# Sample attention: softmax sums from a column of ones, the key norms' root on GpSimd, latent products half a step later

## Chip, cores and metric

The kernel runs on one core of one Trainium2 chip. The metric is the device time of one execution in microseconds; the number of record is the median of several runs. The engines are named as in the profile: PE (TensorE matmul), DVE (VectorE), ACT (ScalarE), POOL (GpSimd), SP (SyncE, which issues the DMAs).

## What is computed

One inference step of a two-layer decoder for a prompt of 1024 tokens and for a sample group of 8 batches of 8 new tokens. The change lies almost wholly in one stage of layer 0, the attention of the sample group over its paged cache: per batch 16 pages of 128 keys, each key a latent row of 256 numbers and a rotary part of 32, and 8 heads with 8 queries each.

```python
def mla_core(qn, qr, k_nope, k_rope, c, mask, w_uv):
    s = (einsum('bqhd,bkhd->bhqk', qn, k_nope)
         + einsum('bqhr,bkr->bhqk', qr, k_rope)) * SOFTMAX_SCALE
    p = softmax(where(mask, s, -inf), axis=-1)
    lat = einsum('bhqk,bkc->bqhc', p, c)          # c: latent rows, 2048 old and 8 new
    return einsum('bqhc,chv->bqhv', lat, w_uv)
# k_nope = rms_norm(einsum('bkc,chd->bkhd', c, w_uk), g_k_nope): one root per key and head
```

## The kernel before

Products are made to float32's accuracy from pairs of float32r parts: x is split into a high part (a cast) and a low part (x minus the high part), and a product is the sum of three passes (`mm3`, L136).

In `sample_attention` a *page pair* is transposed on PE (`cpt`, L921), its high part `ch` is copied out by ACT (L924) and its low part `cl` made by DVE (L925). For each page `keys` runs 12 matmuls `pk` (L136): six of 256 columns and six of 320, ch and cl against the weights `wqh` and `wql`. ACT squares the keys (`psq`, L954), DVE sums the squares per head (`pss`, L956), and ACT copies the raw scores into `s`. After pages 7 and 15 `scale8` turns the 8 x 8 sums per key into 1 / rms (`rsqrt`), multiplies the scores of eight pages by it (`s<-s,prs`, L964) and adds the rotary scores (`s<-s,pr`, L966), which come from the products `pr` (L939).

`rsqrt` works on 128x64 numbers: `rsx` = ss / n + eps (L115), a first guess by a shift and a subtraction on the bits (`rst` L122, `rsr` L123), then three Newton steps of three DVE ops each (`rsu` L125, `rsu` L126, `rsr` or `prs` L127). Everything of it stands on DVE.

The softmax of batch b runs beside the keys of batch b + 1, dealt out by `slot` over 16 half-steps, q = 0 to 15 (half a page pair each). The maxima `smx` are taken over pages 0 to 7 (L973) and over the rest and the new keys (L980, L981, `soft1`); `soft2` transposes them on PE (`mxt`, L985) and makes a diagonal `sdg`; `soft3` spreads it by a product (`mxb`, L995), subtracts, exponentiates on ACT, splits the weights into `ph` (high and low part, 64 columns each) and sums them over the pages (`ssm`, L1004). `vsplit` splits a page's latent rows into `vh` (ACT, L1012) and `vl` (POOL, L1014; in the last batch mostly DVE) in four buffers in turn, at q = 3 to 11; `latent` adds the products of `ph` with `vh` and `vl` up in one PSUM bank (`lat`, L1027 and L1028), at q = 5 to 13, and the new keys' with `cs_h`, `cs_l`. `lat2` copies the bank to `ls`; `lat3` at q = 15 folds high and low part together (`lo`, two products with `i2`, the doubled identity, L1041), sums `ssm` over partitions by a product with ones (L1042), and DVE takes the reciprocal of 128x64 (`sri`, L1044) and multiplies by it into `latT` (L1046).

Each engine runs its list in order. The lists are set by a scheduler from the order in which the code is written and the dependences between tiles; a wait in a list holds up all that stands behind it on that engine.

Of the kernel before, what the change touches and what calls it, by code (L numbers as in the profile page):

```python
# [10 lines left out]
F32 = mybir.dt.float32  # L11
# [75 lines left out]
def wunit(g, ap, a, b, ring, lo=None):  # L87
    """One [128, a, b] block of a weight, split into two float32r parts that add up to it."""
# [10 lines left out]
def wcols(g, w, c0, c1, ring):  # L99
    """Columns c0:c1 of a [1024, n] weight as one unit of eight row blocks."""  # L100
    return wunit(g, w[:, c0:c1].rearrange("(k p) m -> p k m", p=P), KB, c1 - c0, ring)


def rsqrt(g, out, ss, inv_n, n, p=P):
    """out = (ss * inv_n + EPS) ** -0.5 on [p, n], to float32's accuracy."""
    v = g.nc.vector
    x = g.tiny.tile([P, 64], F32, name="rsx", tag="rsx")[:p, :n]
    t = g.tiny.tile([P, 64], I32, name="rst", tag="rst")[:p, :n]
# [13 lines left out]
    v.tensor_single_scalar(t, x.bitcast(I32), 1, ALU.logical_shift_right)  # L122
    v.tensor_scalar(r.bitcast(I32), t, -1.0, float(0x5F3759DF), ALU.mult, ALU.add)  # L123
# [6 lines left out]
def mm3(g, ps, pairs):  # L130
    """Accumulate float32 products of split operands: ((wh, wl), (xh, xl)) per row block."""
# [8 lines left out]
# ------------------------------------------------------------------ constants  # L140
# [19 lines left out]
def bcast_cols(g, ps, dg, r, out, n):  # L160
    """out[:, t * 128 + q] = r[q, t] on every partition: columns of per-token numbers as one row."""
# [7 lines left out]
# ------------------------------------------------------------------ feature-major norm  # L169
# The next product runs on x * gain; the row of 1 / rms, one number per token, multiplies its result.  # L170
# [48 lines left out]
# ------------------------------------------------------------------ MLP  # L219
# [46 lines left out]
class OutProj:  # L266
    """y += w.T @ X per chunk, then the operands and the scale of the next product."""
# [46 lines left out]
def in_even(g, I, O, S, st_left):  # L314
# [3 lines left out]
    with ExitStack() as st:  # L318
# [90 lines left out]
        def zproc(ci, tb0, nb, zs, sq):  # L409
# [34 lines left out]
            # latent and rotary key  # L444
# [12 lines left out]
            else:  # L457
                nc.sync.dma_start(O["ckv_s"][0].rearrange("b t d -> (b t) d"), cn[:p, 0])
                nc.sync.dma_start(O["kr_s"][0].rearrange("b t d -> (b t) d"), kr[:, 0])
                split(g, S.cs_h[:p], S.cs_l[:p], cn[:p, 0])  # L460
# [72 lines left out]
def pool_mixer(g, I, O, S, X, rs0, w, ps, ut, keep):  # L533
# [46 lines left out]
        # trailing window sums by doubling, the last group in two pieces  # L580
# [65 lines left out]
# ------------------------------------------------------------------ layer 0: keys and values  # L646
# [160 lines left out]
# ------------------------------------------------------------------ layer 0: sample attention  # L807
def sample_attention(g, I, S, ahead, fill_start, fill):
    nc = g.nc
    SQ = H * DT  # L810
    with ExitStack() as st:
# [17 lines left out]
        def load(b, pr):  # L829
            """Two pages of batch b."""  # L830
# [16 lines left out]
        # queries, feature-major  # L847
# [6 lines left out]
        # absorbed queries  # L854
# [13 lines left out]
        # moving operand [w_uk | absorbed queries], two copies in turn  # L868
# [6 lines left out]
        # block-diagonal rotary queries for four pages at once  # L875
# [52 lines left out]
        def ropes(b, q):  # L928
            """Rotary scores of pages 4 q .. 4 q + 3."""
# [12 lines left out]
        def keys(b, pg):  # L942
            """Keys of one page: sums of squares per head, and scores by absorbed queries."""
# [24 lines left out]
        mxs, ph_, sm_, pl_ = {}, {}, {}, {}  # L968
# [23 lines left out]
        def soft3(b, dg):  # L992
# [16 lines left out]
        def vsplit(b, pg):  # L1009
            ch = sa.tile([P, R], F32R, name="vh", tag="vh", bufs=4)  # L1010
            c_l = sa.tile([P, R], F32R, name="vl", tag="vl", bufs=4)
            nc.scalar.copy(ch, cps[b, pg])  # L1012
            e = nc.vector if b == DB - 1 and pg % 4 else nc.gpsimd
            e.tensor_tensor(c_l, cps.pop((b, pg)), ch.bitcast(F32), ALU.subtract)  # L1014
            vs[b, pg] = (ch, c_l)

        def latent(b, pg):
# [9 lines left out]
            nc.tensor.matmul(pl[:, :R], w, vh, start=(pg == 0), stop=False)  # L1027
# [4 lines left out]
        def lat2(b):  # L1032
            ls = sa.tile([P, R], F32, name="ls", tag="ls")
            nc.scalar.copy(ls, pl_.pop(b)[:, :R])
            lss[b] = ls

        def lat3(b):
            ls = lss.pop(b)
            po = msc("lo")
            for k in range(2):  # L1040
                nc.tensor.matmul(po[:, k * SQ:(k + 1) * SQ], ls[:, k * P:(k + 1) * P], i2, start=True, stop=True)  # L1041
            nc.tensor.matmul(po[:, 2 * SQ:3 * SQ], g.ones, sm_.pop(b), start=True, stop=True)  # L1042
            ri = sa.tile([P, SQ], F32, name="sri", tag="sri")
            nc.vector.reciprocal(ri, po[:, 2 * SQ:3 * SQ])  # L1044
            for k in range(2):
                nc.vector.tensor_tensor(latT[:, k, :, b * DT:(b + 1) * DT], po[:, k * SQ:(k + 1) * SQ].rearrange("p (h t) -> p h t", t=DT),  # L1046
                                        ri.rearrange("p (h t) -> p h t", t=DT), ALU.mult)

        def slot(b, q):
            """What the batch before does in half-step q (0..15) of the next one."""  # L1050
# [23 lines left out]
        for J in range(NJ + 8):  # L1074
# [31 lines left out]
            slot(b - 1, 2 * pr + 1)  # L1106
        fill()
# [11 lines left out]
# ------------------------------------------------------------------ layer 0: operands of the output projection  # L1119
# [44 lines left out]
def residual(g, y, xts, tb):  # L1164
    """The input's rows of one token block, feature-major."""
# [50 lines left out]
def rnn_prep(g, I):  # L1216
    """Vectors per channel and states, feature-major."""
# [49 lines left out]
def rnn(g, I, O, S, X, RS, gs, rp):  # L1267
    """gs[c][:, n] = gelu(gate) * h for every channel block n."""
# [11 lines left out]
    # the tiles that are free first come last in the pool, where the next phase's weights lie  # L1280
# [339 lines left out]
```

## Time and profile before

| | us |
|---|---|
| median of 3 runs | 2839.73 |
| lowest and highest run | 2837.73, 2841.03 |
| span of the profiled execution | 2838.5 |
| PE busy in it | 2713.7 (96%) |
| DVE, ACT, POOL busy | 1807.2, 898.8, 396.8 |

The sample attention takes the stretch from about 417 to 787 us of the span. Views by stretch (windows) give each engine's busy time in a piece of it; the groups by line say what an engine waited for just before an instruction; the timeline gives starts and durations of single instructions, and in brackets the idle time before one with what ended it. A matmul's duration includes its pipeline's depth, so what PE does per pass is read from the distance between starts, not from durations.

### The profile page before, as it was taken

Reading aid. Unit: us, or ns where it says so; the run is one execution under the profiler, and the core shown is the slowest. Engines: PE = TensorE matmul, PEld = TensorE weight load, DVE = VectorE, ACT = ScalarE, POOL = GpSimd, SP = SyncE. Lnnn points to the kernel's source line nnn. Section 1 sums busy time; section 2 is a strip of 40 time slices with the busy share of each in tenths; the row PEclk is TensorE's granted clock in tenths of the full one; section 3 lists DMA queues with packets and bytes.
Section 4 is the critical chain, followed back from the end, with each engine's and each line's share of the span. In section 5 each row is a group of like instructions: output and inputs, shape, how many; then the busy total and the mean of one; then the engine's idle time right before and its main releaser. Section 6 shows DMA issues by size and latency. Waiting matters only on the chain.

```text
span 2838.5 us, 43000 instructions
## 1 busy us (share of the span) xinstructions
PE 2713.7 (96%) x16801; PEld 2632.6 (93%) x16801; DVE 1807.2 (64%) x3501; ACT 898.8 (32%) x1878; POOL 396.8 (14%) x453
## 2 busy tenths in 40 slices
PE   7998999999999999999999998987999999999999
PEld 6887989888899999999999988887999999999998
DVE  7665657888755555555555579998365555555555
ACT  5334555666634111111111146655321111111111
POOL 4321001232212000000000044555200000000000
PEclk9999998999999999999999999998999999999999
DMA  5233102222251111111111121113111111111111
GB/s 161 62 108 108 38 16 76 62 61 59 70 136 42 45 45 46 42 49 39 49 40 48 36 90 35 35 31 109 47 47 50 39 48 39 49 38 51 38 38 64
DMA packets 200743, 162.07 MB, mean 57 GB/s; under 512 B 40331, under 2 KB 183148, under 8 KB 199763
## 3 DMA queue, kind: packets, MB, share of 16 engines
q1 hardware_dynamic: 200539, 159.31, 18.9%
q8 instruction: 133, 2.18, 0.3%
q14 instruction: 71, 0.58, 0.1%
HBM read 138.18 MB, written 21.21 MB: 56 GB/s over the span
## 4 chain that ended last, share of the span: by engine, by line
PE 62%; DVE 8%; ACT 1%; DMA 1%; POOL 1%; issue 1%; ACTq 0%; DVEq 0%; POOLq 0%
PE up L136 26%; PE dn L136 26%; PE op L136 6%; PE pgt L136 2%; DVE hs L1372 1%; DVE xl L182 1%; PE pg L136 1%; PE pu L136 1%; DVE v L1339 1%; DVE ta L1362 1%; DVE q L1392 0%; DVE y L250 0%; DVE vl L80 0%; ACT whA L79 0%; PE nbc L165 0%
## 5 line engine op out<-in xcount | busy, mean ns | idle before, releaser
L250 DVE TENSOR_TENSOR y<-y,dn 128x384 f32<-128x384 f32 (+1 forms) x768 | 404.9, 531 | 282.0 <-PE dn L136 279.7
L136 PE MATMUL dn<-hh,whB 128*128 128x384 f32 (+1 forms) x1536 | 505.8, 329 | 3.9 <-DVE y L250 3.8
L136 PE MATMUL up<-xh,wlA 128*128 128x384 f32 (+1 forms) x1536 | 501.6, 327 | 0.0
L136 PE MATMUL up<-xh,whA 128*128 128x384 f32 (+1 forms) x1536 | 501.1, 326 | 0.0
L136 PE MATMUL dn<-hh,wlB 128*128 128x384 f32 (+1 forms) x1536 | 501.0, 326 | 0.0
L136 PE MATMUL up<-xl,whA 128*128 128x384 f32 (+1 forms) x1536 | 501.0, 326 | 0.0
L136 PE MATMUL dn<-hl,whB 128*128 128x384 f32 (+1 forms) x1536 | 500.7, 326 | 0.0
L79 ACT CAST whB<-raw 128x1024 fp32r<-128x1024 f32 (+3 forms) x80 | 79.9, 1034 | 703.5 <-PE dn L136 663.4
L136 PEld LDWEIGHTS dn<-hh,whB 128*128 128x128 f32 x1536 | 288.3, 188 | 11.8 <-DVE y L250 11.6
L136 PEld LDWEIGHTS up<-xh,wlA 128*128 128x128 f32 x1536 | 288.3, 188 | 0.4
L136 PEld LDWEIGHTS up<-xh,whA 128*128 128x128 f32 x1536 | 288.3, 188 | 0.3
L136 PEld LDWEIGHTS dn<-hl,whB 128*128 128x128 f32 x1536 | 288.4, 188 | 0.1
L136 PEld LDWEIGHTS up<-xl,whA 128*128 128x128 f32 x1536 | 288.3, 188 | 0.2
L136 PEld LDWEIGHTS dn<-hh,wlB 128*128 128x128 f32 x1536 | 288.3, 188 | 0.0
L235 DVE SCALAR_TENSOR_TENSOR rl<-up,rs 128x384 f32<-128x384 f32 (+1 forms) x192 | 102.8, 535 | 260.3 <-PE up L136 260.3
L236 ACT ACTIVATE hh<-rl 128x384 fp32r<-128x384 f32 (+1 forms) x192 | 97.1, 506 | 447.7 <-DVE rl L235 447.7
L80 POOL TENSOR_TENSOR wlA<-raw,whA 128x1024 fp32r<-128x1024 f32 (+2 forms) x24 | 58.4, 2435 | 769.2 <-ACT whA L79 766.7
L136 PE MATMUL pk<-wqh,cl 128*128 128x256 f32 (+1 forms) x512 | 153.3, 305 | 12.7 <-DVE cl L925 12.6
L136 PE MATMUL pk<-wqh,ch 128*128 128x320 f32 (+1 forms) x512 | 160.1, 315 | 0.7 <-ACT ch L924 0.7
L79 ACT CAST whA<-raw 128x1024 fp32r<-128x1024 f32 (+2 forms) x94 | 98.0, 1042 | 184.8 <-PE up L136 143.2
L237 DVE TENSOR_TENSOR rl<-rl 128x384 f32<-128x384 f32 (+1 forms) x192 | 106.0, 552 | 77.5 <-ACT hh L236 77.5
L136 PE MATMUL pk<-wql,ch 128*128 128x256 f32 (+1 forms) x512 | 151.9, 298 | 1.2 <-DVE wql L80 1.2
(558 smaller groups left out, 5378.5 us busy)
## 6 DMA issues: line engine op xcount, KB each, us to landing
raw<-in_w_up_dram SPq DMA_DIRECT2D x64, 512.0 KB
raw<-in_w_down_dram SPq DMA_DIRECT2D x64, 512.0 KB
cp<-in_cache_ckv_dram SPq DMA_DIRECT2D x128, 128.0 KB
raw<-in_w_in_rnn_dram SPq DMA_DIRECT2D x16, 512.0 KB
xt<-in_x_prompt_dram SPq DMA_DIRECT2D x8, 512.0 KB
raw<-in_w_out_even_dram SPq DMA_DIRECT2D x8, 512.0 KB
raw<-in_x_prompt_dram SPq DMA_DIRECT2D x8, 512.0 KB
raw<-in_w_out_rnn_dram SPq DMA_DIRECT2D x8, 512.0 KB
```

The lines of the kernel that those rows point to most:

```text
L79: g.nc.scalar.copy(h, src)
L80: (lo or g.nc.vector).tensor_tensor(l, src, h.bitcast(F32), ALU.subtract)
L136: g.nc.tensor.matmul(ps, a, b, start=(i == 0), stop=(i == n - 1))
L182: nc.vector.scalar_tensor_tensor(xl[:, m], yv, gcol[:, m:m + 1], xh[:, m].bitcast(F32), ALU.mult, ALU.subtract)
L235: nc.vector.scalar_tensor_tensor(r[:, :n], ps[:, :n], 0.0, RS[c][:, :n], ALU.max, ALU.mult)
L236: nc.scalar.activation(hh[:, a:b], r[:, :n], AF.Square)
L237: nc.vector.tensor_tensor(r[:, :n], r[:, :n], r[:, :n], ALU.mult)
L250: nc.vector.tensor_tensor(y[c][:, m], y[c][:, m], ps[:, :n], ALU.add)
L1339: V.scalar_tensor_tensor(v, ul[:, a + k:b + k], vec[:, k, n:n + 1], v, ALU.mult, ALU.add)
L1362: V.scalar_tensor_tensor(ta[:, a:b], a0[:, a:b], 1.0, ta[:, a:b], ALU.add, ALU.mult)
L1372: V.tensor_tensor_scan(hs[:, a:b], a0[:, a:b], ig[:, a:b], hs[:, a - 1:a] if a else 0.0, ALU.mult, ALU.add)
```

## The change

- `rsqrt`: the shift and the subtraction on the bits become one op (`rsr` from `rsx`, a multiplication by -0.5 and an addition), for all its users. With an engine given, as `scale8` does, the three Newton steps are made of four ops each on GpSimd (three products and one op that scales and adds), 12 in all, since there the op with two operations and two tensors is not used.
- Softmax sums: the tiles of the latent rows' high parts get two columns of ones (`VT`, four fixed pairs of tiles in turn, filled once; `cs_h` likewise), so the `lat` products of `vh` have 258 columns, and the last two hold the sums of the weights. The reduction `ssm` and its product with ones go. `lat3` folds the sums by a small product (`lf`, with the new constant `fold`), takes a reciprocal of 128x1 and scales the doubled identity by it (`i2s`). The folding products `lo` then use `i2s`, in a new step `lat4` at q = 2 of the batch after, with one copy into `latT` in place of two products on DVE.
- Times: `latent` runs at q = 6 to 14 (before 5 to 13) and is written ahead of `vsplit`, now at q = 4 to 11 (before 3 to 11); `lat2` at 14 (before 13).

```diff
+    v.tensor_scalar(r.bitcast(I32), x.bitcast(I32), -0.5, float(0x5F3759DF), ALU.mult, ALU.add)
+    if eng is not None:
+        for it in range(3):
+            eng.tensor_tensor(u, r, r, ALU.mult)
+            eng.tensor_tensor(u, u, x, ALU.mult)
+            eng.tensor_scalar(u, u, -0.5, 1.5, ALU.mult, ALU.add)
+            eng.tensor_tensor(out if it == 2 else r, u, r, ALU.mult)
+        return
...
-            rsqrt(g, r, ss, 1.0 / QN, 64)
+            rsqrt(g, r, ss, 1.0 / QN, 64, eng=nc.gpsimd)
...
-            sm = sa.tile([P, SQ], F32, name="ssm", tag="ssm")
-            nc.vector.tensor_reduce(sm, s.rearrange("p a q -> p q a"), AX.X, ALU.add)
...
+            ch, c_l = vs[b, pg] = VT[pg % 4]
+            nc.scalar.copy(ch[:, :R], cps[b, pg])
...
-            nc.tensor.matmul(pl[:, :R], w, vh, start=(pg == 0), stop=False)
+            nc.tensor.matmul(pl[:, :R + 2], w, vh, start=(pg == 0), stop=False)
...
+            nc.tensor.matmul(pf[:, :2], fold.rearrange("p a q -> p (a q)"), lss[b][:, R:], start=True, stop=True)
+            ri = g.tiny.tile([P, 1], F32, name="sri", tag="sri", bufs=2)
+            nc.vector.reciprocal(ri, pf[:, 0:1])
+            i2s = sa.tile([P, NS], F32, name="i2s", tag="i2s")
+            nc.vector.tensor_scalar_mul(i2s, i2, ri)
...
+                nc.tensor.matmul(po[:, k * SQ:(k + 1) * SQ], ls[:, k * P:(k + 1) * P], i2s, start=True, stop=True)
+            nc.vector.tensor_copy(latT[:, :, :, b * DT:(b + 1) * DT],
+                                  po[:, :2 * SQ].rearrange("p (k h t) -> p k h t", k=2, t=DT))
...
+            if q == 2 and b >= 1:
+                lat4(b - 1)
...
-            if 5 <= q <= 13:
-                for pg in range(2 * (q - 5), 2 * (q - 5) + 2):
+            if 6 <= q <= 14:
+                for pg in range(2 * (q - 6), 2 * (q - 6) + 2):
```

The scheduler then sets other lists. DVE in the middle of a batch, before (Newton chain from `rsx` on; `cl` is the low part of pair 29's latents, which PE waits for):

```order
L925 TENSOR_TENSOR cl<-cpt,ch 128x512
L956 TENSOR_REDUCE pss<-psq 128x8
L115 TENSOR_SCALAR rsx<-pss 128x64
L122 TENSOR_SCALAR rst<-rsx 128x64
L123 TENSOR_SCALAR rsr<-rst 128x64
L125 TENSOR_TENSOR rsu<-rsr 128x64
L126 SCALAR_TENSOR_TENSOR rsu<-rsu,rsx 128x64
L127 SCALAR_TENSOR_TENSOR rsr<-rsu,rsr 128x64
L956 TENSOR_REDUCE pss<-psq 128x8
L125 TENSOR_TENSOR rsu<-rsr 128x64
L925 TENSOR_TENSOR cl<-cpt,ch 128x512
```

The same place in the list of the changed kernel:

```order
L938 TENSOR_TENSOR cl<-cpt,ch 128x512
L969 TENSOR_REDUCE pss<-psq 128x8
L114 TENSOR_SCALAR rsx<-pss 128x64
L122 TENSOR_SCALAR rsr<-rsx 128x64
L969 TENSOR_REDUCE pss<-psq 128x8
L977 TENSOR_TENSOR s<-s,prs 128x512
L938 TENSOR_TENSOR cl<-cpt,ch 128x512
L979 TENSOR_TENSOR s<-s,pr 128x512
```

The steps between `rsr` and the product have left DVE's list, and the product that needs their result now stands ahead of the second `cl`.

POOL's list there, in the changed kernel (the last Newton step, then the low parts of pages 8 and on; before, the list held `vl` alone there):

```order
L125 TENSOR_TENSOR rsu<-rsr 128x64
L126 TENSOR_TENSOR rsu<-rsu,rsx 128x64
L127 TENSOR_SCALAR rsu<-rsu 128x64
L128 TENSOR_TENSOR prs<-rsu,rsr 128x64
L1024 TENSOR_TENSOR vl_4920<-cp,vh_4919 128x256
L1024 TENSOR_TENSOR vl_4922<-cp,vh_4921 128x256
```

So the low parts behind the chain run only when it is done; those of pages 4 to 7 stand ahead of it.

PE at the boundary between two batches, before: the transposed maxima `mxt` stand among the `cpt` transposes of the fourth page pair of the next batch, behind 62 `pk` passes of it:

```order
L136 MATMUL pk<-wqh_4916,cl 128x320
L921 MATMUL cpt<-ident,cp 128x128 x3
L985 MATMUL mxt<-ident,smx 64x128
L921 MATMUL cpt<-ident,cp 128x128
L136 MATMUL pk<-wqh_4916,cl 128x256
```

And in the changed kernel, in the middle of the fourth page, behind 45 `pk` passes:

```order
L142 MATMUL pk<-wqh_4891,ch 128x320
L142 MATMUL pk<-wql_4892,ch 128x320
L142 MATMUL pk<-wqh_4891,cl 128x320
L998 MATMUL mxt<-ident,smx 64x128
L142 MATMUL pk<-wqh_4891,ch 128x320
L142 MATMUL pk<-wql_4892,ch 128x320
```

`mxt` moved ahead by 17 `pk` passes and three transposes.

## Rows read from the trace of the kernel before

**Rows 1.** The page's head and its first part: busy time, share of the span and instructions of each engine.

```profile
span 2838.5 us, 43000 instructions
...
PE 2713.7 (96%) x16801; PEld 2632.6 (93%) x16801; DVE 1807.2 (64%) x3501; ACT 898.8 (32%) x1878; POOL 396.8 (14%) x453
```

**Rows 2.** Timeline of PE at the transposed maxima of one batch (start, duration, engine, line, operation, operands).

```profile
568.18 0.30 PE L985 MATMUL mxt<-ident,smx 128*64 128x128 f32 x1
```

**Rows 3.** Windows of some 41 us in the stage: stretch and its length, then busy time and count of PE, PE's weight loads, DVE, ACT and POOL, the granted clock of PE, the DMA share and GB/s.

```profile
566.00:607.00 41.00, 38.47 (x277) 35.72 (x276) 33.91 (x67) 26.20 (x83) 12.21 (x18) 1.00 0.23 59
```

**Rows 4.** Groups of PE's instructions by line in one batch, 568.18 to 609.70: busy time, mean ns | idle time just before them and what ended it.

```profile
L136 PE MATMUL pk<-wqh,cl 128*128 128x256 f32 (+1 forms) x64 | 19.0, 302 | 1.5 <-DVE cl L925 1.5
...
L1028 PE MATMUL lat<-vl,ph 128*128 128x256 f32 x16 | 4.5, 302 | 0.8 <-POOL vl L1014 0.7
...
L985 PE MATMUL mxt<-ident,smx 128*64 128x128 f32 x2 | 0.6, 298 | 0.3
```

**Rows 5.** Timeline of PE in that batch, around its middle and at its end (in brackets idle time before, and what ended it).

```profile
577.28 0.28 PE L1027 MATMUL lat<-vh,ph 128*128 128x256 f32 x1
578.25 0.39 PE L1028 MATMUL lat<-vl,ph 128*128 128x256 f32 x1 [0.70 <-POOL vl L1014]
...
582.71 0.28 PE L1028 MATMUL lat<-vl,ph 128*128 128x256 f32 x1
582.83 0.28 PE L1027 MATMUL lat<-vh,ph 128*128 128x256 f32 x1
...
583.30 0.28 PE L136 MATMUL pk<-wql,ch 128*128 128x256 f32 x1
585.13 0.39 PE L136 MATMUL pk<-wqh,cl 128*128 128x256 f32 x1 [1.55 <-DVE cl L925]
...
598.64 0.59 PE L939 MATMUL pr<-qbd,kpT 128*128 128x256 f32 x2
599.08 0.55 PE L1041 MATMUL lo<-i,ls 128*128 128x64 f32 x4
...
599.66 0.36 PE L136 MATMUL pk<-wqh,ch 128*128 128x256 f32 x1
...
601.34 0.60 PE L921 MATMUL cpt<-ident,cp 128*128 128x128 f32 x4
601.70 0.36 PE L136 MATMUL pk<-wqh,ch 128*128 128x256 f32 x1
...
606.57 0.31 PE L136 MATMUL pk<-wqh,ch 128*128 128x320 f32 x1
...
609.70 0.30 PE L985 MATMUL mxt<-ident,smx 128*64 128x128 f32 x1
```

**Rows 6.** Timeline of DVE in the middle of the batch.

```profile
578.14 0.67 DVE L956 TENSOR_REDUCE pss<-psq 128x8 f32<-128x512 f32 x1
578.84 0.43 DVE L115 TENSOR_SCALAR rsx<-pss 128x64 f32<-128x64 f32 x1
579.31 2.93 DVE L122 TENSOR_SCALAR rst<-rsx 128x64 int32<-128x64 int32 x1
...
584.39 0.68 DVE L925 TENSOR_TENSOR cl<-cpt,ch 128x512 fp32r<-128x512 f32 x1
...
586.49 0.22 DVE L127 SCALAR_TENSOR_TENSOR prs<-rsu,rsr 128x64 f32<-128x64 f32 x1
```

**Rows 7.** Timeline of POOL beside it.

```profile
579.36 2.82 POOL L1014 TENSOR_TENSOR vl<-cp,vh 128x256 fp32r<-128x256 f32 x4
```

**Rows 8.** Timeline of DVE behind the last batch: the second op of the first Newton guess, the first and the last of nine Newton ops that follow each other undisturbed, the last maximum, the sums of the weights.

```profile
765.03 0.18 DVE L122 TENSOR_SCALAR rst<-rsx 128x64 int32<-128x64 int32 x1
...
765.48 0.23 DVE L125 TENSOR_TENSOR rsu<-rsr 128x64 f32<-128x64 f32 x1
...
767.55 0.23 DVE L127 SCALAR_TENSOR_TENSOR prs<-rsu,rsr 128x64 f32<-128x64 f32 x1
...
777.02 2.11 DVE L1004 TENSOR_REDUCE ssm<-s 128x64 f32<-128x1088 f32 x1
```

**Rows 9.** One line of layer 1 on POOL, a product of two tensors of 128x64: least, median and greatest duration in ns, first and last start.

```profile
L1398 POOL TENSOR_TENSOR y<-q,hs x8: 305/617/636, 1758.0 to 1960.2; 128x64 f32<-128x64 f32 x8
```

**Rows 10.** Group of POOL's copies of the new keys' scores (busy us, mean ns | idle before).

```profile
L978 POOL COPY s<-snew 64x64 f32<-64x64 f32 x8 | 1.9, 238 | 2.8 <-DVE snew L904 2.7
```

**Rows 11.** Timeline of POOL: two ops on the same tile, one behind the other.

```profile
418.62 0.28 POOL L899 TENSOR_SCALAR_AFFINE_SELECT msk<-msk 64x64 f32<-64x64 f32 x1
418.97 0.28 POOL L900 TENSOR_SCALAR_AFFINE_SELECT msk<-msk 64x64 f32<-64x64 f32 x1
```

**Rows 12.** Timeline of DVE at the boundary between two batches.

```profile
599.26 0.69 DVE L956 TENSOR_REDUCE pss<-psq 128x8 f32<-128x512 f32 x1 [0.35 <-ACT psq L954]
...
605.36 0.69 DVE L964 TENSOR_TENSOR s<-s,prs 128x512 f32<-128x512 f32 x1
...
607.76 1.16 DVE L980 TENSOR_REDUCE smx<-s 128x64 f32<-128x576 f32 x1
...
609.43 0.21 DVE L981 TENSOR_TENSOR smx<-smx 128x64 f32<-128x64 f32 x1
```

**Rows 13.** Timeline of PE behind the last batch, up to its maxima.

```profile
771.23 0.66 PE L1174 MATMUL xtp<-ident,raw 128*128 128x128 f32 x2 [1.60 <-DMA raw<-in_x_prompt_dram]
771.68 0.42 PE L985 MATMUL mxt<-ident,smx 128*64 128x128 f32 x1
```

More of the change, by code (lines that the diff above doesn't have):

```diff
@@ L101, in wcols, with rsqrt @@
     return wunit(g, w[:, c0:c1].rearrange("(k p) m -> p k m", p=P), KB, c1 - c0, ring)
-def rsqrt(g, out, ss, inv_n, n, p=P):
+def rsqrt(g, out, ss, inv_n, n, p=P, eng=None):
     v = g.nc.vector
     x = g.tiny.tile([P, 64], F32, name="rsx", tag="rsx")[:p, :n]
-    t = g.tiny.tile([P, 64], I32, name="rst", tag="rst")[:p, :n]
     u = g.tiny.tile([P, 64], F32, name="rsu", tag="rsu")[:p, :n]
@@ L121, in rsqrt @@
         return
-    v.tensor_single_scalar(t, x.bitcast(I32), 1, ALU.logical_shift_right)
-    v.tensor_scalar(r.bitcast(I32), t, -1.0, float(0x5F3759DF), ALU.mult, ALU.add)
+    v.tensor_scalar(r.bitcast(I32), x.bitcast(I32), -0.5, float(0x5F3759DF), ALU.mult, ALU.add)
[6 more added lines that the diff above has]
+        return
     for it in range(3):
@@ L459, in zproc @@
                 nc.sync.dma_start(O["kr_s"][0].rearrange("b t d -> (b t) d"), kr[:, 0])
-                split(g, S.cs_h[:p], S.cs_l[:p], cn[:p, 0])
+                split(g, S.cs_h[:p, :R], S.cs_l[:p], cn[:p, 0])
+                nc.gpsimd.memset(S.cs_h[:p, R:].bitcast(F32), 1.0)
             later(g, lambda: latents(tb0, nb, p, cn))
@@ L887, in sample_attention @@
         nc.vector.tensor_copy(i2[NS:], g.ident[NS:, NS:])
+        fold = sa.tile([P, 2, NS], F32, name="fold", bufs=1)
+        nc.gpsimd.tensor_copy(fold, i2[:, None, :].to_broadcast([P, 2, NS]))
+        VT = [(sa.tile([P, R + 2], F32R, name=f"vh{i}", bufs=1), sa.tile([P, R], F32R, name=f"vl{i}", bufs=1)) for i in range(4)]
+        for vh, _ in VT:
+            nc.gpsimd.memset(vh[:, R:].bitcast(F32), 1.0)
         latT = sa.tile([P, 2, H, NS], F32, name="latT", bufs=1)
@@ L966, in scale8 @@
             nc.vector.tensor_tensor(sf, sf, pr8[b].rearrange("p a q -> p (a q)"), ALU.add)
-        mxs, ph_, sm_, pl_ = {}, {}, {}, {}
+        mxs, ph_, pl_ = {}, {}, {}
         HF = ((0, 8), (8, NPG + 1))
@@ L1002, in soft3 @@
                 nc.vector.tensor_tensor(ph[:, x:y, 1], sv, ph[:, x:y, 0].bitcast(F32), ALU.subtract)
-            sm = sa.tile([P, SQ], F32, name="ssm", tag="ssm")
-            nc.vector.tensor_reduce(sm, s.rearrange("p a q -> p q a"), AX.X, ALU.add)
-            ph_[b], sm_[b] = ph, sm
+            ph_[b] = ph
         vs = {}
         def vsplit(b, pg):
-            ch = sa.tile([P, R], F32R, name="vh", tag="vh", bufs=4)
-            c_l = sa.tile([P, R], F32R, name="vl", tag="vl", bufs=4)
-            nc.scalar.copy(ch, cps[b, pg])
+            ch, c_l = vs[b, pg] = VT[pg % 4]
+            nc.scalar.copy(ch[:, :R], cps[b, pg])
             e = nc.vector if b == DB - 1 and pg % 4 else nc.gpsimd
-            e.tensor_tensor(c_l, cps.pop((b, pg)), ch.bitcast(F32), ALU.subtract)
-            vs[b, pg] = (ch, c_l)
+            e.tensor_tensor(c_l, cps.pop((b, pg)), ch[:, :R].bitcast(F32), ALU.subtract)
         def latent(b, pg):
@@ L1032, in lat2, with lat4 @@
         def lat2(b):
-            ls = sa.tile([P, R], F32, name="ls", tag="ls")
-            nc.scalar.copy(ls, pl_.pop(b)[:, :R])
+            ls = sa.tile([P, R + 2], F32, name="ls", tag="ls")
+            nc.scalar.copy(ls, pl_.pop(b)[:, :R + 2])
             lss[b] = ls
         def lat3(b):
-            ls = lss.pop(b)
+            pf = msc("lf")
+            nc.tensor.matmul(pf[:, :2], fold.rearrange("p a q -> p (a q)"), lss[b][:, R:], start=True, stop=True)
[3 more added lines that the diff above has]
+            nc.vector.tensor_scalar_mul(i2s, i2, ri)
+            lss[b] = lss[b], i2s
+        def lat4(b):
+            ls, i2s = lss.pop(b)
             po = msc("lo")
             for k in range(2):
[L1041 to L1047, printed above, removed]
+                nc.tensor.matmul(po[:, k * SQ:(k + 1) * SQ], ls[:, k * P:(k + 1) * P], i2s, start=True, stop=True)
+            nc.vector.tensor_copy(latT[:, :, :, b * DT:(b + 1) * DT],
+                                  po[:, :2 * SQ].rearrange("p (k h t) -> p k h t", k=2, t=DT))
         def slot(b, q):
+            if q == 2 and b >= 1:
+                lat4(b - 1)
             if b < 0:
@@ L1056, in slot @@
                 soft3(b, st_.pop(b))
-            if 3 <= q <= 11:
-                for pg in range(2 * (q - 3), min(2 * (q - 3) + 2, NPG)):
-                    vsplit(b, pg)
-            if 5 <= q <= 13:
-                for pg in range(2 * (q - 5), 2 * (q - 5) + 2):
+            if 6 <= q <= 14:
+                for pg in range(2 * (q - 6), 2 * (q - 6) + 2):
                     if pg <= NPG:
                         latent(b, pg)
-            if q == 13:
+            if 4 <= q <= 11:
+                for pg in range(2 * (q - 4), 2 * (q - 4) + 2):
+                    vsplit(b, pg)
+            if q == 14:
                 lat2(b)
@@ L1106, in sample_attention @@
             slot(b - 1, 2 * pr + 1)
+        lat4(DB - 1)
         fill()
@@ L1446, in step @@
         S.kr = l0p.tile([P, NTB, QR], F32, name="kr")
-        S.cs_h = l0p.tile([P, R], F32R, name="cs_h")
+        S.cs_h = l0p.tile([P, R + 2], F32R, name="cs_h")
         S.cs_l = l0p.tile([P, R], F32R, name="cs_l")
```

## Prediction

> **What bounds the kernel now.** I read the page's head first: TensorE (PE) is busy 96% of the span [rows 1], so only stages in which it waits can give or take time. The change touches one stage, the sample attention: 8 batches of 16 pages, about 41.5 us a batch (the transpose `mxt` of one batch stands at 568.18, that of the next at 609.70) [rows 2, 5]. There PE is busy 38.5 of 41 us, VectorE (DVE) 33.9 and GpSimd (POOL) 12.2, at a granted clock of 1.00, the 2.4 GHz level [rows 3]. PE runs its list in order, so a batch is the sum of its passes and of its waits. The groups of one batch name the waits: 1.5 us for DVE's `cl`, 0.7 to 0.8 for POOL's `vl`, 0.3 at the two `mxt` [rows 4]. Matmul starts show a little more: `lat` passes that otherwise follow 0.12 us apart stand 0.97 apart at 578.25, and the `pk` pass on `cl` comes 1.83 after its neighbour at 585.13, 1.7 too late [rows 5]. With smaller hitches of the `lat` passes just before, I put the `vl` waits at 1.7 us, the `cl` wait at 1.7, and at the boundary between batches some 0.4. All that the change can win is therefore about 4 us in each of 7 or 8 batches, near 30 us.
>
> Both larger waits lie in the middle of a batch. DVE gets `rsx` at 578.84; the next Newton step `rst`, 0.2 us of work, takes 2.93 while POOL runs four `vl` (579.36, 2.82 us), and `prs` ends at 586.7. `cl` was put inside this chain and is done only at 585.07 [rows 6, 7].
>
> **The Newton chain on GpSimd** is the term that decides. Two chains a batch (16 in all) lose 10 ops on DVE and get 12 on POOL: 9 with two inputs, 3 with one, each waiting for the one before. On DVE nine steps run from 765.48 to 767.78, 2.30 us [rows 8]. No POOL op of this kind on 128x64 stands in this stage. Nearest is `y<-q,hs` on 128x64: least 305 ns, median 617 [rows 9]; for one input the 64x64 copy with 238 ns [rows 10]. Two dependent POOL ops start 0.35 apart when one takes 0.28, so 0.07 goes to each hand-over [rows 11]. I take the least of 305, since DVE mostly idles while it waits for this chain: 9 x 0.375 + 3 x 0.31 = 4.3 us. Bounds: 12 x 0.31 = 3.7 if all cost as the copy, 12 x 0.69 = 8.2 if all cost the median. The chain is thus some 2 us longer than DVE's undisturbed one.
>
> **The boundary.** Let t count from the `pr` pass behind page 15 (598.64). Before, `pss` is done at 1.3, the product `s<-s,prs` starts at 6.7, since `pss` and `cl` are mixed into the chain, and the last maximum is done at 11.0, 0.06 before `mxt` [rows 5, 12]. After: `pss` 1.3; with the small reciprocal, its scaling, `rsx` and `rsr`, POOL can start at 2.25; chain to 6.6; product, sum, a `pss`, the 1.16 us maximum, a `pss`, the last maximum: 6.65 + 0.7 + 0.7 + 0.6 + 1.1 + 0.6 + 0.2 = 10.5. So `mxt` is ready half a microsecond earlier than before. But in the new order PE reaches it earlier by far: between page 15 and `mxt` stand 45 `pk` passes, where there were 62. Three pages of 1.68, two sets of `cpt` transposes of 0.36 and nine passes more reached 606.57 in the old trace, t = 7.9, and the two `lo` passes fewer bring it to 7.5 [rows 5]. PE waits 3.0 us there, 2.6 more than now. `cl` of the next pair stands behind the last maximum, but only some 0.7 us behind, so it is just in time. The first `lat` may then wait 0.3 for `ph`.
>
> **The middle.** t counts from the end of page 7's products. `pss` to 1.3; POOL still has `vl` of pages 6 and 7 ahead of the chain, whose fixed tiles come free only behind PE's `lat` passes of pages 2 and 3, so it starts at 2.3 to 2.6 and ends at 6.6 to 6.95. DVE's list has the product `s<-s,prs` ahead of `cl`, so `cl` is done at 8.3. PE gets there at 5.7: `pr` 0.5, eleven `lat` passes of 0.12, two pages of 1.68, four `cpt` 0.36 and two passes [rows 5]. It waits 2.55 instead of 1.7. The longer chain stays in this place, in front of the same matmul. The `vl` of pages 8 and on are queued behind the chain on POOL; their first reader stands a page behind the late `cl` (9.8 against 7.7), so that costs nothing unless the chain grows by 2 us.
>
> **What is taken away.** Latents half a step later and tiles with fixed turns: the `vl` wait of 1.7 us should go, since `vl` of pages 4 to 7 now run ahead of the chain and PE asks later. The 2.11 us reduction `ssm` leaves DVE [rows 8], as do the two reciprocals' worth of work at the boundary; on DVE only the part before a `cl` counts, and the waits above have it already. PE saves two passes a batch, 0.2 us. Constants and four fills of ones: once, on an idle POOL, nothing; `lat` passes of 258 columns for 256: 17 x 1 ns, nothing; one op fewer in nine other roots: under 0.2 us each, beside matmuls.
>
> **The tail.** Behind the last batch the POOL chain is on the path, 1.4 to 2 us longer, but PE waits 1.60 for a DMA just ahead of `mxt` [rows 13], and without `ssm` the last `vl` and `lat` come 2 us earlier; the extra pass through `lf`, reciprocal and `lo` gives 1 back. I take +0.5, from -1 to +1.5.
>
> **The sum**, against the profiled execution: span 2838.5 [rows 1], 1.2 below the median 2839.73. Boundary 7 x 2.6 = +18.2; `ph` 7 x 0.3 = +2.1; middle 8 x 0.85 = +6.8; `vl` 7 x 1.7 = -11.9; PE passes -1.4; tail +0.5: **+14.3 us**, 2852.8 of span, 2854 as a median. Every microsecond of the chain counts in both places of nearly every batch, 15 us. It comes out even at a chain of 3.35 us, 0.28 an op with its hand-over.
>
> **Rivals.**
> *The POOL chain is short, or PE's new place fits it (faster, 2828).* At 2.6 us, DVE's pace, the sum is 14.3 - 1.7 x 15 = -11. For it: the rough spans of POOL, and a DVE that is relieved of 4 us a batch, so that `cl` and `pss` come earlier everywhere. Against it: no two-input row under 305 ns. The floor, with all waits gone, is near 2810.
> *It cancels (within 0.2%, 2840).* A chain of 3.7 us, the lower bound, gives 14.3 - 9 = +5, just inside; likewise if the 2.93 us hold of `rst` was costlier than I count.
> *POOL and DVE hinder each other (slower, 2872 and more).* `y<-q,hs` takes 617 ns in its median, and `rst` shows the reverse case. If the first third of each chain, beside `pss` and `cl`, runs at the median, the chain grows by 4 x 0.31 = 1.2 us: +18, 2872. From a chain of 6.3 us on, `vl` is late as well, and the waits it was to lose return: 2890.
> *A step's rule.* At 64 columns POOL takes 305 ns where DVE takes 225 [rows 8, 9], 1.36 times as long. If it were twice as long, 9 x (0.45 + 0.07) + 3 x 0.31 = 5.6 us of chain give 14.3 + 1.3 x 15 = +34, 2874. The Trainium skill ("GPSIMD Engine Reference", 4.1 Engine selection) says just that, GpSimd about two times slower than VectorE for elementwise work with two inputs, and that such work belongs on VectorE; the least of the row above speaks for a milder factor at this width.
> *It does nothing,* since the stage is not on the path: nothing runs beside PE's list that could hide its waits, so this has no chance of its own and lies in the even case.
>
> **How the numbers follow.** Forecast case (2844 to 2864) 0.43; engines that hinder each other 0.12, the factor of two 0.10; even 0.14; faster 0.21. Slower than 2845.4, that is by over 0.2%, about what a measurement of this kernel can tell from no change: 0.65. Same 0.14, faster 0.21. The range leaves out the extremes of the dear cases and the deep end of the faster one: 2827 to 2875.
>
> **What would show it.** Right: PE groups with a wait of about 3 us at `mxt` and 2.5 at `cl`, both a batch, released by DVE; `vl` gone from PE's releasers; a chain of 12 POOL ops over 4.3 us; the last maximum at t = 10.5; a period near 43.5 us. Wrong: POOL steps under 0.28 us, or above 0.45; `mxt` with no wait (then the new order was well placed, and the kernel is faster by the `vl` waits alone); new waits for `vl` at pages 8 to 11, or for `lo`.

## The result, and the profile after

The changed kernel takes **2872.24 us** (median of 4 runs, 2871.3 to 2875.18), the kernel before 2838.73 beside it (4 runs, 2837.24 to 2841.03): ratio **1.0121, 95% interval 1.0106 to 1.0135**, 33.5 us slower. Slower was forecast, and 2872 lies in the range, near its end; the size was more than double the forecast of 14.3.

| | before | after |
|---|---|---|
| span of the profiled execution | 2838.5 us | 2869.5 us |
| mean granted clock of PE over the span | 0.976 | 0.969 |
| from `mxt` to `mxt`, the batch of [rows 2] | 41.52 us | 47.61 us |
| idle of PE before `mxt`, 8 of them | 0.9 us | 22.1 us |
| idle of PE before `pk` on `cl`, whole span | 12.7 us | 22.4 us |
| idle of PE before `lat` on `vl`, whole span | 5.3 us | 0.7 us |

The page's head and its first part, after, beside [rows 1]:

```profile
span 2869.5 us, 43004 instructions
...
PE 2716.9 (95%) x16801; PEld 2642.4 (92%) x16801; DVE 1750.7 (61%) x3324; ACT 897.7 (31%) x1878; POOL 452.7 (16%) x651
```

PE's busy time rose by 3.2 us although the number of its instructions is the same (two `lf` products of a batch stand where two products with ones stood): something made passes longer. The groups of PE over the whole span, before and then after (idle time of PE just before the group, and what ended it):

```profile
L136 PE MATMUL pk<-wqh,cl 128*128 128x256 f32 (+1 forms) x512 | 153.3, 305 | 12.7 <-DVE cl L925 12.6
L1028 PE MATMUL lat<-vl,ph 128*128 128x256 f32 x128 | 35.9, 302 | 5.3 <-POOL vl L1014 3.7 <-DVE vl L1014 0.9
L985 PE MATMUL mxt<-ident,smx 128*64 128x128 f32 x8 | 2.5, 311 | 0.9 <-DVE smx L981 0.3
```

```profile
L142 PE MATMUL pk<-wqh,cl 128*128 128x256 f32 (+1 forms) x512 | 160.2, 316 | 22.4 <-DVE cl L938 22.4
L1037 PE MATMUL lat<-vl,ph 128*128 128x256 f32 x128 | 37.0, 309 | 0.7 <-POOL vl L1024 0.5
L998 PE MATMUL mxt<-ident,smx 128*64 128x128 f32 x8 | 2.9, 360 | 22.1 <-DVE smx L994 22.1
```

So the `vl` waits went, and two larger ones stand in their place, both ended by DVE. The timeline of PE around them, to be held against [rows 5] (start, duration, operands; in brackets idle time before):

```profile
591.95 0.58 PE L142 MATMUL pk<-wqh,cl 128*128 128x256 f32 x1 [2.87 <-DVE cl L938]
592.33 0.41 PE L142 MATMUL pk<-wqh,ch 128*128 128x256 f32 x1
592.54 0.41 PE L142 MATMUL pk<-wql,ch 128*128 128x256 f32 x1
...
608.53 0.59 PE L952 MATMUL pr<-qbd,kpT 128*128 128x256 f32 x2
...
618.91 0.42 PE L998 MATMUL mxt<-ident,smx 128*64 128x128 f32 x1 [2.75 <-DVE smx L994]
618.99 0.61 PE L142 MATMUL pk<-wqh,ch 128*128 128x320 f32 x1
619.40 0.47 PE L142 MATMUL pk<-wql,ch 128*128 128x320 f32 x1
```

Read not only the brackets but the passes behind them: the 128x256 passes follow 0.21 us apart, where the kernel before has 0.12. The windows of these places name the reason (busy times, then the granted clock, ahead of the DMA share and GB/s):

```profile
588.80:592.00 3.20, 0.34 (x4) 0.13 (x2) 1.90 (x3) 0.76 (x3) 2.95 (x7) 0.90 0.04 14
592.00:594.50 2.50, 2.50 (x10) 2.50 (x11) 2.04 (x3) 0.38 (x1) 1.26 (x2) 0.50 0.37 103
...
619.00:621.50 2.50, 2.50 (x12) 2.50 (x13) 1.59 (x4) 0.75 (x3) 0.00 (x0) 0.50 0.00 0
```

0.50 is the 1.2 GHz level: PE was idle for most of 3 us, and the passes behind ran at half rate. The kernel before waits 1.55 us at the first place [rows 5] and its passes behind run at 1.00.

The chain itself, on POOL (its first step, and its last op with the four `vl` queued behind it), and DVE beside it, to be held against [rows 6, 12]:

```profile
585.61 0.29 POOL L125 TENSOR_TENSOR rsu<-rsr 128x64 f32<-128x64 f32 x1
585.99 0.32 POOL L126 TENSOR_TENSOR rsu<-rsu,rsx 128x64 f32<-128x64 f32 x1
586.39 0.25 POOL L127 TENSOR_SCALAR rsu<-rsu 128x64 f32<-128x64 f32 x1
586.72 0.33 POOL L128 TENSOR_TENSOR rsr<-rsu,rsr 128x64 f32<-128x64 f32 x1
...
589.75 0.32 POOL L128 TENSOR_TENSOR prs<-rsu,rsr 128x64 f32<-128x64 f32 x1
590.02 3.24 POOL L1024 TENSOR_TENSOR vl<-cp,vh 128x256 fp32r<-128x256 f32 x4
```

```profile
590.10 1.20 DVE L977 TENSOR_TENSOR s<-s,prs 128x512 f32<-128x512 f32 x1 [3.21 <-POOL prs L128]
591.22 0.68 DVE L938 TENSOR_TENSOR cl<-cpt,ch 128x512 fp32r<-128x512 f32 x1
...
615.10 0.69 DVE L977 TENSOR_TENSOR s<-s,prs 128x512 f32<-128x512 f32 x1 [2.37 <-POOL prs L128]
...
618.64 0.21 DVE L994 TENSOR_TENSOR smx<-smx 128x64 f32<-128x64 f32 x1
```

From 585.61 to 590.07 the chain takes 4.46 us; 4.3 was forecast. Meanwhile DVE stands 3.21 us before the product `s<-s,prs`, and `cl`, which needs nothing from the chain, stands behind it in DVE's list.

### The profile page after: what moved, and what is told of

Read it like the earlier page. It is cut to its first block, busy times and chain, and to the rows that moved or that the text cites. A ratio compares the mean times of both kernels' runs of the same rounds, so it can differ in the third digit from the quotient of the medians.

```text
span 2869.5 us, 43004 instructions
## 1 busy us (share of the span) xinstructions
PE 2716.9 (95%) x16801; PEld 2642.4 (92%) x16801; DVE 1750.7 (61%) x3324; ACT 897.7 (31%) x1878; POOL 452.7 (16%) x651
## 4 chain that ended last, share of the span: by engine, by line
PE 61%; DVE 8%; ACT 1%; issue 0%; POOL 0%; DMA 0%; ACTq 0%; DVEq 0%; SPq 0%; POOLq 0%
PE up L142 26%; PE dn L142 26%; PE op L142 6%; PE pgt L142 1%; DVE hs L1390 1%; DVE xl L188 1%; DVE v L1357 1%; PE pu L142 1%; PE pg L142 1%; DVE ta L1380 1%; DVE q L1410 0%; DVE vl L80 0%; DVE y L256 0%; PE otp L1569 0%; DVE t L1372 0%
## 5 line engine op out<-in xcount | busy, mean ns | idle before, releaser
L142 PE MATMUL pk<-wqh,cl 128*128 128x256 f32 (+1 forms) x512 | 160.2, 316 | 22.4 <-DVE cl L938 22.4
L142 PE MATMUL pk<-wqh,ch 128*128 128x320 f32 (+1 forms) x512 | 168.9, 331 | 0.7 <-ACT ch L937 0.7
L142 PE MATMUL pk<-wql,ch 128*128 128x256 f32 (+1 forms) x512 | 159.7, 313 | 1.4 <-DVE wql L80 1.4
```

Source lines behind the costliest of these rows:

```text
L142: g.nc.tensor.matmul(ps, a, b, start=(i == 0), stop=(i == n - 1))
```

## The experiments

The theory: the chain on GpSimd costs all of the time, and each long wait behind it costs more than its length, by passes at half rate. The rivals: the rest of the change costs something of its own; the place of `mxt` in PE's list is the cost, or that of `cl` in DVE's list; a wait that is mended in one place comes up in another, since the chain holds DVE wherever its readers stand. (In the texts on record the theory is A; B is the rest of the change, C the place of `mxt`, D the wait that moves on, E a chain that costs its length wherever its readers stand, F another cause of the slow passes.) Each run is set against the kernel before on the same chip.

**e1: the changed kernel, the chain back on VectorE.**

```diff
-            rsqrt(g, r, ss, 1.0 / QN, 64, eng=nc.gpsimd)
+            rsqrt(g, r, ss, 1.0 / QN, 64)
```

> The changed kernel with one part undone: the three Newton steps run on VectorE again (nine ops, the two first ops stay merged); ones columns, late latents and fixed tiles stay. Theory A (the GpSimd chain of 4.46 us makes TensorE wait 2.8 us at mxt and 3.0 us at cl in every batch, and after waits of that length TensorE's granted clock falls and the next dozen passes run at half rate): both long waits shrink below 1.7 us, no fall of the clock in the middle of a batch, period 41 to 42 us, time 2828 to 2845. Theory B (the late latents, fixed tiles or the two-step folding cost the time): 2858 to 2875, period still 45 or more.

Measured: 2828.63 against 2836.51, ratio 0.9966 (0.9953 to 0.998); the time between `mxt` and `mxt` is 40.17 us. `mxt` waits for nothing, and the `cl` wait is that of the kernel before:

```profile
581.88 0.39 PE L142 MATMUL pk<-wqh,cl 128*128 128x256 f32 x1 [1.55 <-DVE cl L938]
```

So the rest of the change gains 7.9 us, and the chain costs more than the whole loss.

**e2: the kernel before, with the chain alone on GpSimd** (the same lines, and `eng` in `rsqrt` as in the diff).

```diff
-            rsqrt(g, r, ss, 1.0 / QN, 64)
+            rsqrt(g, r, ss, 1.0 / QN, 64, eng=nc.gpsimd)
```

> The kernel before with one part of the change alone: Newton steps of the key norms on GpSimd (12 ops), all else as before. Theory A: waits of 2.5 to 3.5 us at mxt and at cl with a fall of the clock behind them, plus the old wait for vl; 2865 to 2885. Theory B: at most 2850.

Measured: 2873.7 against 2836.51, ratio 1.0122 (1.0102 to 1.0142), as much as the whole change. Here the waits of one batch lie in three places, all ended by DVE:

```profile
606.25 0.67 PE L947 MATMUL pr<-qbd,kpT 128*128 128x256 f32 x2 [1.26 <-DVE s L974]
...
608.45 0.39 PE L144 MATMUL pk<-wqh,cl 128*128 128x256 f32 x1 [0.82 <-DVE cl L933]
...
627.68 0.30 PE L993 MATMUL mxt<-ident,smx 128*64 128x128 f32 x1 [2.56 <-DVE smx L989]
```

**e3: the changed kernel with one Newton step on GpSimd for three.** Two steps of the root are left out, so its time is that of a chain of 4 ops for 12, some 3.0 us shorter by the 0.37 us an op of the trace.

```diff
-        for it in range(3):
+        for it in range(2, 3):
```

> The changed kernel with one Newton step on GpSimd instead of three (the root is then less exact: two steps of the root are left out), so the chain has 4 ops and takes 1.5 us instead of 4.46. Theory A: mxt and cl waits together under 2 us a batch, no fall of the clock, 2825 to 2842. Theory B: 2855 to 2872. Theory C (the place of mxt in TensorE's list costs, whatever the chain's length): wait at mxt stays above 2 us, 2850 to 2860.

Measured: 2821.03 against 2836.51, ratio 0.9937 (0.9918 to 0.9956); 40.0 us a batch, and 0.26 us of wait at `mxt` between batches. It is a little faster than expected. Against the changed kernel that is 51 us for 3.0 us of chain, 17 us for each of them, where the sum had 15. GpSimd itself does no harm; the length of the chain does.

**e4: the changed kernel, the product `s<-s,prs` of the middle behind `cl` in DVE's list** (`issue_after` puts what it encloses behind the named instruction).

```diff
+        def apply8(b, g8):
+            r = rr.pop((b, g8))
             s8 = sc[b][:, g8 * 8:g8 * 8 + 8]
...
+                if pr == 5:
+                    with g.tc.issue_after(CL[b, 5].ins):
+                        apply8(b, 0)
```

> The changed kernel with one order pinned on VectorE: in the middle of a batch the product with the roots (s<-s,prs) stands behind the cl of the next page pair instead of ahead of it; the GpSimd chain is as long as before. Theory A (a wait is made by what the chain holds up, and the fall of the clock comes behind the wait): the 3.03 us wait for cl and the slow passes behind it go, the 2.8 us wait at mxt stays; period about 42.5 us, 2835 to 2848. Rival D (VectorE, held at the product, then keeps the sums of squares and with them TensorE's banks): the wait shows up again a page later, 2860 to 2872.

Measured: 2844.88 against 2837.9, ratio 1.0026 (1.0016 to 1.0036): 26.5 us of the 33.5 come back. The `cl` wait is gone, that at `mxt` stays at 2.75. The stage then shows what a wait costs beside its length, since batches of 41.9 and 43.4 us alternate with the same wait. The two `mxt`, the windows of the 2.5 us behind them, apart:

```profile
562.11 0.30 PE L1007 MATMUL mxt<-ident,smx 128*64 128x128 f32 x1 [2.75 <-DVE smx L1003]
...
605.47 0.30 PE L1007 MATMUL mxt<-ident,smx 128*64 128x128 f32 x1 [2.76 <-DVE smx L1003]
```

```profile
562.40:564.90 2.50, 2.50 (x16) 2.50 (x14) 1.38 (x4) 1.14 (x4) 0.00 (x0) 0.58 0.06 12
605.80:608.30 2.50, 2.50 (x19) 2.12 (x17) 1.63 (x5) 1.11 (x4) 0.00 (x0) 1.00 0.07 11
```

Behind the first the clock falls to 0.58 and the next 16 passes take 2.96 us; behind the second they take 2.05 at full rate. What tells the two apart was not found.

**e5: e4, and `mxt` behind page 4 of the next batch** (60 `pk` passes for 45, about the place it had before; the steps behind it, up to `ph`, start later with it).

```diff
+            if b < DB - 1 and q == 4:
+                with g.tc.issue_after(PK[b + 1, 3][-1].ins):
+                    st_[b] = soft2(b)
```

> As e4, and mxt pinned behind the fourth page of the next batch, 60 pk passes behind the boundary instead of 45; the GpSimd chain unchanged. Theory A: wait at mxt about 1.2 us instead of 2.8, none at cl, no fall of the clock; period 40 to 41 us, 2820 to 2835. Theory E (a chain of 4.46 us costs its length wherever its readers stand): above 2850.

Measured: 2847.78, ratio 1.005 (1.0031 to 1.007): no gain, the expectation missed. The wait at `mxt` is gone, but a new one stands ahead of it:

```profile
567.26 0.39 PE L142 MATMUL pk<-wqh,cl 128*128 128x256 f32 x1 [1.94 <-DVE cl L940]
```

`cl` of the next pair is queued on DVE behind the product and the maxima that wait for the chain. So the early place of `mxt` is not the cause; a later one only shows the next matmul that waits for DVE. That is what the rivals D and E say of the boundary.

**e6: e4, with 16 transposes of no use just ahead of `mxt`,** to keep PE busy in the wait.

```diff
+            for _ in range(16 if b < DB - 1 else 0):
+                w = nc.tensor.transpose(pt[:, P:2 * P], g.ident, g.ident)
```

> As e4, and 16 transposes of a constant into unused columns of the mxt bank stand directly ahead of mxt (48 pk passes behind the boundary): 1.8 us more TensorE work in each of 7 batches, of no use, in time in which TensorE waits anyway. Theory A (behind a wait of some 2.8 us the clock falls and costs about 1.3 us more): wait at mxt under 1 us, no slow passes behind it, 6 to 11 us faster than e4. Rival F (the slow passes come from elsewhere, or the length of the wait has no part in them): within 3 us of e4.

Measured: 2843.31, ratio 1.0025 (1.0015 to 1.0035). By the time it fits rival F, 1.6 us from e4, but it decides nothing: the transposes waited themselves 1.59 us for their bank, so they did not fill the wait.

```profile
605.80 1.97 PE L1003 MATMUL mxt<-ident 128*128 128x128 f32 x16 [1.59 <-DVE latT L1068]
```

**e7: e1, the middle's root and product behind `cl`.**

```diff
+                    ss0 = ss8[b]
+                if pr == 5:
+                    with g.tc.issue_after(CL[b, 5].ins):
+                        scale8(b, 0, ss0)
```

> As e1 (Newton steps on VectorE, all else of the change kept), and the roots of the first eight pages start behind the cl of the next page pair. Theory A: the wait for cl of 1.7 us, the last long one in a batch of e1, goes; 2812 to 2822. Rival D: it moves to another reader of VectorE; 2826 to 2832.

Measured: 2825.0, ratio 0.996 (0.9946 to 0.9974), no better than e1, so the theory's expectation is missed. As rival D has it, the wait moved to the next batch half's products, whose bank is freed only by the sum behind the root:

```profile
579.59 0.70 PE L954 MATMUL pr<-qbd,kpT 128*128 128x256 f32 x2 [1.77 <-DVE s L982]
```

**e8: the changed kernel, 20 transposes of no use in the middle, meant to stand ahead of the pass on `cl`.**

```diff
+                pw = one("wrm", "ms")
+                for _ in range(20):
+                    w = nc.tensor.transpose(pw[:, :P], g.ident, g.ident)
```

> The changed kernel with its orders kept, and in the middle of each batch 20 transposes of a constant into an unused bank directly ahead of the pk pass that waits 3.03 us for cl: 2.2 us of TensorE work of no use in each of 8 batches, in time in which it waits anyway. Theory A (behind a wait of some 3 us the granted clock falls, and the passes behind it cost about 1.5 us more): wait at cl under 1 us, the 16 passes behind it take 2.15 us instead of 3.4 to 3.9; 8 to 14 us faster than the changed kernel, ratio to the kernel before 1.007 to 1.0095. Rival F (slow passes have another cause): within 3 us of the changed kernel, ratio 1.011 to 1.0135.

Measured: 2886.89, ratio 1.0184 (1.0167 to 1.0201). It says nothing of the theory: the scheduler put them behind the waiting pass (wait at 604.81, `wrm` from 605.51), so they came on top.

```profile
604.81 0.64 PE L144 MATMUL pk<-wqh,cl 128*128 128x320 f32 x1 [2.56 <-DVE cl L943]
605.51 0.84 PE L967 MATMUL wrm<-ident 128*128 128x128 f32 x3
```

**e9: e7, with the products copied out of their bank by ScalarE,** so that DVE's sum no longer holds the bank.

```diff
+                    if pr == 3 or pr == 7 and b < DB - 1:
+                        prc[b] = sk.tile([P, 512], F32, name="prc", tag="prc", bufs=1)
+                        nc.scalar.copy(prc[b], pr8[b].rearrange("p a q -> p (a q)"))
```

> As e7 (Newton steps on VectorE, roots behind cl), and ScalarE copies the rotary scores pr out of their bank, so that TensorE's next pr need not wait for the sum on VectorE (in e7 it waits 1.8 us there). Theory A: that wait goes too; period 38.6 to 39.2 us, 2808 to 2818. Rival D: it moves on once more; 2822 or more.

Measured: **2811.09** against 2833.41, ratio **0.9924 (0.9907 to 0.9941)**, faster than both kernels. PE is busy 40.05 of 41 us at a clock of 1.00, and in a batch of 38.8 a wait of 0.62 us is left beside one of 0.33:

```profile
575.97 0.38 PE L142 MATMUL pk<-wqh,cl 128*128 128x256 f32 x1 [0.62 <-DVE cl L940]
```

**e10: e4, with the same copy, the last maximum behind `cl` of the next batch's third pair and `mxt` behind page 5,** the most room that could be given to the chain on GpSimd.

```diff
+            with g.tc.issue_after(CL[b + 1, 2].ins) if b < DB - 1 else nullcontext():
+                nc.vector.tensor_reduce(mx[:, 1], s[:, 8:].rearrange("p a q -> p q a"), AX.X, ALU.max)
...
+            if b < DB - 1 and q == 5:
+                with g.tc.issue_after(PK[b + 1, 4][-1].ins):
+                    st_[b] = soft2(b)
```

> Newton steps on GpSimd as in the changed kernel, chain of 4.46 us, but every reader given room: in the middle the product stands behind cl, pr is copied out by ScalarE, at the boundary the last maximum stands behind the cl of the third page pair and mxt behind the fifth page. Theory A (the chain costs only by what stands behind it): waits over 0.6 us gone but for one of about 1 us at the boundary's cl, no fall of the clock; 2812 to 2828. Theory E (a chain of this length costs wherever its readers stand): above 2840.

Measured: 2851.66, ratio 1.0065 (1.0048 to 1.0082), worse than e4: the theory's expectation (2812 to 2828) is missed and rival E's (above 2840) met. The products, sums and maxima behind the chain still stand ahead of some `cl`:

```profile
596.37 0.39 PE L142 MATMUL pk<-wqh,cl 128*128 128x256 f32 x1 [2.18 <-DVE cl L940]
```

No run with the whole chain on GpSimd came under the kernel before; whether another placing of its readers would is not shown.

**e11: e8 mended,** with the orders of DVE and PE else kept, so that the 20 transposes stand directly ahead of the waiting pass.

```diff
+                with g.tc.issue_after(g.mm[-1].ins):
+                    pw = one("wrm", "ms")
+                    for _ in range(20):
+                        WM[b] = nc.tensor.transpose(pw[:, :P], g.ident, g.ident)
```

> As e8, whose transposes came to stand behind the waiting pass; now every other pass keeps its place and the 20 transposes stand directly ahead of the pk pass that waits for cl. Theory A: wait at cl 0.5 to 1.2 us, the 16 passes behind it take about 2.15 us instead of 3.4 to 3.9 in most batches; 8 to 14 us faster than the changed kernel, ratio to the kernel before 1.007 to 1.0095. Rival F: passes behind it as slow as before, ratio 1.011 to 1.0135.

Measured: 2858.18 against 2834.99, ratio 1.0092 (1.0073 to 1.0111): 23.2 us over the kernel before, where the changed kernel has 33.5, although PE does 2.4 us more work in each batch. DVE is as late as before; the passes behind it now run at full rate:

```profile
590.27 2.40 PE L966 MATMUL wrm<-ident 128*128 128x128 f32 x20 [0.53 <-ACT kpT L954]
592.60 0.38 PE L144 MATMUL pk<-wqh,cl 128*128 128x256 f32 x1
592.82 0.28 PE L144 MATMUL pk<-wqh,ch 128*128 128x256 f32 x1
592.94 0.28 PE L144 MATMUL pk<-wql,ch 128*128 128x256 f32 x1
```

```profile
592.60:595.10 2.50, 2.50 (x21) 2.50 (x21) 2.50 (x4) 1.23 (x5) 1.33 (x2) 1.00 0.42 112
```

The seven times between `mxt` and `mxt` sum to 309.7 us, against 323.2 in the changed kernel: 13.5 us, 1.9 a batch. That is about the price of the half rate at this one place: the profiled run, 2855.35, is among the faster of the six (2854.66 to 2865.9), and by the medians 10.3 us come back. The intervals of the two ratios just touch, from 1.0106 to 1.0111.

## Why the prediction was right in direction and wrong in size

**The step that failed is the sum.** "Boundary 7 x 2.6; ... middle 8 x 0.85" priced each wait at its own length and had no term for the passes behind it. The trace shows a second price: where PE had been idle for most of 3 us, its granted clock was mostly 0.50 behind it, and the passes there took longer. In the kernel before, the 16 passes behind the `cl` wait take 2.15 us; in the changed one 3.4 to 3.9, and over seven middles that adds 10.75 us. Behind `mxt` it happens in about half of the batches, and adds 4.5. These 15.3 us are the first 16 passes alone, and the low clock outlasts them: in the middle shown above it stands until 598.2, 6 us. The windows from the first `mxt` to the last, the kernel before and then the changed one, hold all of it:

```profile
484.16:771.68 287.52, 266.71 (x1919) 248.48 (x1919) 236.10 (x462) 183.59 (x570) 82.98 (x121) 1.00 0.22 58
```

```profile
480.25:803.49 323.24, 280.44 (x1925) 268.77 (x1925) 181.66 (x315) 184.18 (x572) 132.32 (x289) 0.92 0.20 54
```

A mean of 0.92 is some 51 us at half rate. Passes 0.21 us apart for 0.12 lose 0.43 of such time, 22 us, and a little of it lies in the waits themselves; so by estimate about 20 us are no wait at all. e11 took the fall behind `cl` away and with it 13.5 us, and e4 shows 1.5 us a batch between two batches with the same wait. The Trainium skill ("TensorE: Matmul & The Clock Gate", section "HAM oscillation — how this bites in real kernels") describes the mechanism: matmuls that waits interrupt again and again are throttled between them, and the low clock is paid in the matmuls that follow. The two windows at 0.50 agree; e4's alternating batches show that not each wait of 2.75 us brings a fall.

The rest of the sum, term by term, from the two traces:

| term | forecast | measured |
|---|---|---|
| boundary, `mxt` waits | +18.2 | +18.2 (the first seven, 0.9 to 19.1) |
| `ph` | +2.1 | +0.7 |
| middle, `cl` wait | +6.8 | +9.7 (idle 12.7 to 22.4) |
| `vl` waits | -11.9 | -7.1 (by starts, 1.4 in each of five batches) |
| passes fewer | -1.4 | none: PE has 16801 instructions in both |
| tail | +0.5 | +0.5 (`mxt` +3.0, the DMA wait ahead of it 3.3 to 1.6, the rest -0.8) |
| passes at half rate behind the waits | none | about +20 (estimate; the first 16 passes alone +15.3) |
| set-up ahead of the stage | none | -5.8 |
| sum | +14.3 | about +36, where the span grew by 31.0 |

The 5 us left over lie in small differences between matmul starts that no idle time shows; they were not taken apart.

**The chain** was priced right: 4.46 us for 4.3, with ops of 0.29 to 0.33 and 0.25 us. Both rivals that end near 2872 are wrong in their reason, though not in their time: at the chain's first ops, beside `pss` and `cl`, the POOL ops took 0.29 and 0.32 us, not the 617 ns of [rows 9], and 0.32 for DVE's 0.23 is a factor of 1.4. That the measured time lies where these rivals put it is chance. The factor of two of the Trainium skill ("GPSIMD Engine Reference", 4.1 Engine selection) does not hold at this width.

**The boundary** was right: the last maximum is done at t = 10.3 for 10.5, PE arrives at 7.6 for 7.5, and waits 2.75 for 3.0. That PE's earlier place made this wait is true of this list only: e5 moved `mxt` back and DVE's `cl` waited in its stead.

**The middle** was undersized. The order was as forecast, but the product took 1.20 us for the 0.69 that it takes at the boundary, while POOL ran its four `vl` from 590.02, so `cl` was later and the wait 2.87 for 2.55. It took 1.19 to 1.20 in seven middles and 0.69 in the first, where POOL has no `vl`: so here POOL's work goes with a longer DVE product, not with a longer chain.

**The `vl` term** had nearly the right size a batch and too many batches. From one `lat` start to the next, a batch before sums to 5.08 us in five batches and to 3.54 in e1, so 1.4 to 1.5 us went where 1.7 were forecast; in the first and the last of the seven the `lat` passes had not waited. Of this the groups of PE count only 0.8 as idle [rows 4]. **The passes** were miscounted: this term took two off a batch and left out the two of `lf` that come in their place. With the chain at DVE's pace the forecast was -11; e1, which has it there, gains 7.9.

**Open.** Ahead of the stage the changed kernel gains 5.8 us. There the clock stood at 0.50 from 420 to 424 in the kernel before and at 1.00 in the changed one, with the same kind of passes:

```profile
420.00:424.00 4.00, 4.00 (x24) 3.30 (x24) 1.26 (x4) 1.16 (x2) 0.00 (x0) 0.50 0.42 131
```

```profile
420.00:424.00 4.00, 4.00 (x43) 3.66 (x42) 1.50 (x5) 2.13 (x5) 1.22 (x9) 1.00 0.41 131
```

The change does not account for it: e1 and e8, which have the changed kernel's set-up, stand at 0.50 from 422 to 426 like the kernel before, and e3, e4 and e9 at 1.00. What decides it in a run was not found; without it the changed kernel's trace is 36.8 us longer. Nor did a run separate the half rate behind `mxt` from its wait, since e6 did not fill that wait.

## What to carry to other kernels

Price a wait of the bound engine as its length plus what the passes behind it take at the granted clock that follows; here a wait of 1.55 us cost its length, and the 13.5 us of e11, over seven waits of 2.9 us, are about two thirds as much again. A chain of small dependent operations that moves to another engine does not free the first one if the chain's reader stands in its in-order list: move the reader behind whatever the bound engine needs next, and free the buffer that the reader then holds, without which the wait only moves (e7 against e9, both with the chain on DVE). With the chain on GpSimd, one reader moved gave back 26.5 us of 33.5 (e4), and all of them moved gave back less (e10), so there the move is no cure; a chain of a third of the ops was (e3). As long as the chain holds the list, another place for the bound engine's own wait gains nothing (e5).

## What the runs showed of the hardware that was not expected

- Work of no use shortened the kernel: 20 transposes in a wait of 2.9 us kept the granted clock at 1.00 behind it, and 23.2 us of loss stood where 33.5 had stood (e11).
- Waits of equal length, 2.75 and 2.76 us, were followed by a clock of 0.58 and of 1.00 in neighbouring batches (e4); behind one of 2.69 us in e1 it was 1.00.
- POOL's two-input ops of 128x64 took 0.29 to 0.33 us with 0.08 to the next, beside DVE's `pss` and `cl` as without them, while a DVE product of two SBUF tensors took 1.20 us for 0.69 beside POOL's `vl`.
